# Second pass of the input projection: ScalarE copies the products out of PSUM, an accumulating DMA adds the first slab's sums

## The chip, the cores and the metric

The kernel runs on one core of a Trainium2 chip. The metric is the device time of one execution in microseconds. Before the change it was 2701.43 us, the median of 3 runs (2699.49 to 2702.08). The profile is of one more execution, which took 2703.73 us; the span that it shows, from the first to the last instruction, is 2701.6 us. What lies around the span is thus 2.1 us.

Five engines with their own instruction queues take part. Each works through its queue in order, so an instruction that waits holds up everything behind it on that engine. PE is the matrix engine (TensorE), PEld its weight loads, DVE is VectorE, ACT is ScalarE, POOL is GpSimd and SP is SyncE, which here only issues DMAs. Matrix products land in PSUM, eight banks of 128 x 512 floats; everything else lives in SBUF or in DRAM.

## The reference

Two layers of a transformer trunk over 512 latent tokens and 256 context tokens, width 2048, in float32. Each layer normalises and modulates the tokens, projects them with one wide matrix, runs four groups of four attention heads (differential A, windowed B, neighbourhood C, QK-normed D), gates the results, and projects back:

```
n  = rms_norm(h, pre_norm_g[l]) * (1.0 + scale[:, None]) + shift[:, None]
p  = jnp.split(n @ w_in[l], split_points, axis=-1)
pc = jnp.split(nc @ w_in[l], split_points, axis=-1)
oa, oa_c = diff_attention(...); ob, ob_c = window_attention(...)
on, on_c = neighborhood_attention(...); od, od_c = qknorm_attention(...)
y = (jnp.concatenate([oa, ob, on, od], axis=-1) * jax.nn.silu(p[12])) @ w_out[l]
h = h + gate[:, None] * rms_norm(y, post_norm_g[l])
```

`n @ w_in` has an inner length of 2048 and 7168 columns. The kernel handles the columns as 56 blocks of 128: the queries, keys, values and gates of the heads.

## The kernel before, in words

**Two passes.** Of the inner length of 2048, the first half (the first slab, 8 tiles of 128) is multiplied in a first pass for all 56 blocks, two blocks at a time with seven products in place of eight. Its sums go to a DRAM tensor `part[l, b]`, 128 rows x 2 x 384 floats per block: 256 latent and 128 context tokens in each of the two halves. In the second pass (`block_slots`) the second slab is multiplied, block by block, and the first slab's sums are added; the finished block goes at once to what uses it. While the second pass goes on, the attention of heads whose blocks are complete is worked in between (`head_steps`), and so is the modulation of the next layer (`mod_steps`: VectorE's lines 441 and 443, with the tile `mraw` loaded by SP). The two second passes lie at about 508 to 1165 us (layer 0) and 1912 to 2497 us (layer 1).

**Precision.** Each float32 operand is split into a high and a low part: ScalarE copies the high part (line 292), VectorE subtracts it (line 293), and `mm3` multiplies three times (lines 301 to 303). Weights (`wr` split to `wh`, `wl`) are split up to two tiles ahead; the transposed attention weights go the same way (`PTh`, `PTl`).

**A block of the second pass** is 8 slots. In each slot three matmuls add one of 8 tiles to the block's sums for the 512 latent tokens, in PSUM bank 0 or 1 by turns (`self.lb`). The products for the 256 context tokens (`ctx_steps`, bank 2) are run four tiles at a time, in the slots that follow; in layer 1 only keys and values have them. When the last tile is in, VectorE adds the tile `c`, which already holds the sums of the first pass, and leaves the total in `c` (line 819 for the latent part, line 841 for the context part). The tile `c` was loaded from `part` by SP one block ahead (`hold`, line 796).

**What reads `c`.** `done(c, ctx)` is called right behind the addition. It depends on the block: rotary embedding on VectorE (lines 868, 862, 865) for the latent queries and keys of A and B; a permuted copy on ScalarE (line 965) for C; a square and a scaled copy on ScalarE (lines 921, 922) for D; a tanh on ScalarE (line 1017) for gates, of latent and context tokens; splits on ScalarE (lines 278, 282, 292, 295) for the context parts of queries and keys; transposes on PE, three slots later (line 1001), for values.

**What sets the order.** `drive` calls one slot after another and, behind each, the attention and modulation steps that are due; `later(n, fn)` calls a function n slots later. The instructions so written are then put in each engine's queue by a scheduler when the kernel is built, which moves those that it holds for ready ahead of others. What is quoted as order below is each engine's finished queue.

**POOL** has little to do: it adds the neighbourhood bias tables (line 1265, three additions for each C head, after SP has loaded them as `x<-in_rpb`) and a few tiles between the layers. No DMA is issued from it.

Of the kernel before, what the change touches and what calls it, by code (L numbers as in the profile page):

```python
# [10 lines left out]
F32 = mybir.dt.float32  # L11
F32R = mybir.dt.float32r
I32 = mybir.dt.int32
AF = mybir.ActivationFunctionType
ALU = mybir.AluOpType
# [3 lines left out]
P = 128  # L19
# [7 lines left out]
DEPTH = 2  # L27
# [15 lines left out]
HT = 384  # L43
# [12 lines left out]
def lat_of(x):  # L56
    return x[:, :, 0:2 * P]


def ctx_of(x):  # L60
    return x[:, :, 2 * P:HT]
# [16 lines left out]
def fit(ap, like):  # L78

    return ap.rearrange("p (h t) -> p h t", h=like.shape[1]) if len(like.shape) == 3 else ap  # L80


class Kernel:
# [704 lines left out]

        return [lambda m=m, half=half: slot(m, half) for m in order for half in range(2)]

    def hold(self):

        if self.to_hold:
            l, b, w = self.to_hold.pop(0)
            c = self.cp.tile([P, 2, HT], F32, tag="c", bufs=4, name="c")[:, :, 0:w]
            self.nc.sync.dma_start(c, self.part[l, b, :, :, 0:w])
            self.held.append(c)

    def block_slots(self, l, n, what, b):

        with_ctx = l < DEPTH - 1 or what in "kv"
        done = self.take[n, what]
        r = {}

        def slot(c, j):
            if c == 0 and j == 0:
                self.lb ^= 1
                r["c"] = self.held.pop(0)
                self.hold()
            if j == 0:  # L810
                self.cur = self.weight()
            hi, lo = self.cur
            k = 4 * c + j
            js = slice(j * P, (j + 1) * P)
            (th, tl), _ = self.plain(k)
            self.mm3(self.bank(self.lb), hi[:, js], lo[:, js], th, tl, k == 0, k == 7)
            if k == 7:
                lat = lat_of(r["c"])
                self.nc.vector.tensor_add(lat, fit(self.bank(self.lb), lat), lat)  # L819
                done(r["c"], False)  # L820
            if j == 0:
                self.ctx_steps()
            if j == 3:
                self.pend = (hi, lo, c, r["c"], done) if with_ctx else None

        return [lambda c=c, j=j: slot(c, j) for c in range(2) for j in range(4)]

    def ctx_steps(self):

        if self.pend is None:  # L830
            return
        hi, lo, c, tile_c, done = self.pend
        out = self.bank(2, CTX)
        for j in range(4):
            k = 4 * c + j
            js = slice(j * P, (j + 1) * P)
            _, (th, tl) = self.plain(k)
            self.mm3(out, hi[:, js], lo[:, js], th, tl, k == 0, k == 7)
        if c == 1:
            ctx = ctx_of(tile_c)  # L840
            self.nc.vector.tensor_add(ctx, fit(out, ctx), ctx)
            done(tile_c, True)

    def x3(self):
        return self.ap.tile([P, SEQ], F32, tag="x3", bufs=3, name="x3")
# [436 lines left out]
    def layer(self, l):  # L1282

        tc, nc, a = self.tc, self.nc, self.a
        pairs = [(n, i) for n, u in enumerate(self.units) for i in range(len(u[3]))]
        self.tbanks, self.tb = [5, 6], 0
        f = self.first
        before = {1: f[1] + f[2], 6: self.rest + f[6] + f[5], 5: f[7], 7: f[3], 3: f[4]}
        again = self.second(self.ns2)
        slots = []  # L1290
        for p in pairs:
            hooks = (before, {}) if p == pairs[0] else ({}, again) if p == pairs[-1] else None
            slots.append(self.pair_slots(l, *p, START if p == pairs[0] else ORDER, hooks))
        self.drive(slots[0])
        if l == 0:
            self.heads_setup()
        anchors = [i.ins for i in self.anchors]

        def behind(fn):
            with tc.issue_after(anchors[0]), tc.issue_after(anchors[1]):  # L1300
                fn()

        self.drive([x for s in slots[1:-1] for x in s], [lambda fn=fn: behind(fn) for fn in self.late])
        self.drive(slots[-1])
        self.flush()
        self.stage.close()

        self.att = ExitStack()
        self.ap = self.att.enter_context(tc.tile_pool(name=f"att{l}", bufs=1, reuse_waits="tile"))
        self.mp, self.raws, self.og_open = Lent(self), 3, False  # L1310
        self.load_cst("rope_sub")
        self.take, sts = {}, {}
        for n in range(len(self.units)):
            self.unit_blocks(l, n, sts)
        self.held, self.lb, self.pend = [], 0, None
        self.to_hold = []
        for n, i in pairs:
            blocks = self.units[n][3][i]
            wide = l < DEPTH - 1 or blocks[0][0] == "k"
            self.to_hold += [(l, b, HT if wide else 2 * P) for _, b in blocks]  # L1320
        self.hold()
        mods = self.mod_steps([(l, 2, c, (0, 1) if l < DEPTH - 1 else (0,)) for c in range(4)])
        steps, left, last = [], 0, 0
        for n, (kind, h, gh, prs) in enumerate(self.units):
            if h == 0 and kind == "D":
                self.later(7, lambda: self.load_cst("rope_head"))
            if h == 0 and kind == "B":
                self.bm = self.ap.tile([P, 256], F32, tag="qd", bufs=2, name="bmask")
                nc.sync.dma_start(self.bm, a["bmask"])
            if h == 0 and kind == "C":  # L1330
                self.later(7, lambda: self.na_bias(l, 0))

            goal = left - last * (0 if n == len(self.units) - 1 else 0.25 if len(prs) > 1 else 0.6)
            now, done = [], 0
            while steps and done < goal:
                now.append(steps.pop(0))
                done += now[-1][0]
            left -= done
            nm = 0 if n < 6 else len(mods) * len(prs) // sum(len(u[3]) for u in self.units[n:])
            ms, mods = mods[:nm], mods[nm:]  # L1340
            self.drive([x for p in prs for w, b in p for x in self.block_slots(l, n, w, b)], now, ms)
            new = [x if isinstance(x, tuple) else (1, x) for x in self.head_steps(l, kind, h, gh, sts[n])]
            last = sum(w for w, _ in new)
            if n == 0:
                new.insert(0, (0.4 * last, lambda: None))
            left += sum(w for w, _ in new)
            steps += new
        self.ctx_steps()
        self.pend = None
        self.flush()  # L1350
        self.raws, self.og_open = RAWS, True
        self.tbanks, self.tb = [5], 0
        self.backlog = [fn for _, fn in steps]
# [259 lines left out]
```

## Time and profile before

| | |
|---|---|
| median of 3 runs | 2701.43 us (2699.49 to 2702.08) |
| profiled execution, its span | 2703.73 us, 2701.6 us |
| PE busy | 2591.7 us, 96% |
| DVE busy | 2187.2 us, 81% |
| ACT busy | 1285.7 us, 48% |
| POOL busy | 43.6 us, 2% |
| DMA issued by SP, moved | 408.45 MB |

The page's shares are averages over the whole span; what the second pass does is read from windows. A matmul's time overlaps the next one's, so PE can read as busy while it is not at its peak. A row "X <- Y: a, b, c" of the view of waits says that X sat idle a us in total, b times, c us at most, until Y ended.

### The profile page before, as it was taken

How to read it: one execution, taken by the hardware profiler on the slowest of the kernel's cores; microseconds unless marked ns; L12 is line 12 of the kernel's file. 1: busy time of each engine (PE TensorE's matmuls, PEld its weight loads, DVE VectorE, ACT ScalarE, POOL GpSimd, SP SyncE). 2: the span in 40 equal slices, each digit the busy share in tenths (PEclk: the TensorE clock that was granted, in tenths of full speed). 3: DMA queues.
4: the chain of work that ended last, by engine and by line, in shares of the span. 5: the costliest groups of instructions: out<-in, count | busy, mean ns of one | idle time of the engine just before them, and what ended most of it. 6: DMA issues, size and time to landing. Idle time of an engine off the chain costs nothing.

```text
span 2701.6 us, 41385 instructions
## 1 busy us (share of the span) xinstructions
PE 2591.7 (96%) x14392; PEld 2231.2 (83%) x14392; DVE 2187.2 (81%) x4480; ACT 1285.7 (48%) x2532; POOL 43.6 (2%) x42
## 2 busy tenths in 40 slices
PE   7899999999999999999999689999999999999997
PEld 1799999987888888887777479999878887888885
DVE  4899998789899888767889989887798988876524
ACT  3534343445556455546533464444455554544422
POOL 0000000000000000000010000000000000000001
PEclk9899999999999999999999789999999999999998
DMA  9455554422223334427886535444422334444632
GB/s 318 138 197 194 196 196 149 151 73 78 85 96 116 119 126 142 140 89 232 293 269 218 201 123 170 148 146 137 152 87 86 112 121 136 146 154 129 223 103 98
DMA packets 230497, 411.09 MB, mean 152 GB/s; under 512 B 25568, under 2 KB 59664, under 8 KB 229776
## 3 DMA queue, kind: packets, MB, share of 16 engines
q1 hardware_dynamic: 230288, 408.45, 46.3%
q8 instruction: 113, 1.85, 0.3%
q14 instruction: 96, 0.79, 0.1%
HBM read 348.17 MB, written 60.19 MB: 151 GB/s over the span
## 4 chain that ended last, share of the span: by engine, by line
PE 76%; DVE 11%; DMA 7%; ACT 3%; issue 2%; SPq 0%; POOL 0%; DVEq 0%; ACTq 0%; POOLq 0%
PE ps L301 23%; PE ps L302 23%; PE ps L303 22%; DMA mraw<-in_w_mod 3%; PE ps L1132 3%; DVE macc L443 2%; DVE wl L293 1%; PE ps L650 1%; PE ps L1034 1%; DMA mr<-in_w_mod 1%; DVE rt L862 1%; DVE h L1442 1%; PE ps L1035 1%; DMA wr<-in_w_out 1%; DMA wr<-ogd 1%
## 5 line engine op out<-in xcount | busy, mean ns | idle before, releaser
L301 PE MATMUL ps<-arena,wh 128*128 128x384 f32 (+2 forms) x3104 | 1050.6, 339 | 16.6 <-ACT arena L292 7.4
L302 PE MATMUL ps<-arena,wh 128*128 128x384 f32 (+2 forms) x3104 | 1038.8, 335 | 0.0
L303 PE MATMUL ps<-arena,wl 128*128 128x384 f32 (+2 forms) x3104 | 1037.7, 335 | 0.0
L292 ACT ACTIVATE wh<-wr 128x512 fp32r<-128x512 f32 x696 | 437.8, 630 | 710.1 <-PE ps L302 371.3
L301 PEld LDWEIGHTS ps<-arena,wh 128*128 128x128 f32 x3104 | 586.9, 189 | 47.5 <-ACT arena L292 8.6
L293 DVE TENSOR_TENSOR wl<-wr,wh 128x512 fp32r<-128x512 f32 x696 | 477.4, 688 | 176.3 <-ACT wh L292 163.7
L303 PEld LDWEIGHTS ps<-arena,wl 128*128 128x128 f32 x3104 | 587.0, 189 | 33.0
L302 PEld LDWEIGHTS ps<-arena,wh 128*128 128x128 f32 x3104 | 587.8, 189 | 27.4 <-DVE arena L293 1.1
L443 DVE SCALAR_TENSOR_TENSOR macc<-mraw,sc,macc 128x512 f32<-128x512 f32 x540 | 391.2, 750 | 38.3 <-DMA mraw<-in_w_mod 37.6
L302 PE MATMUL ps<-wl,arena 128*128 128x512 f32 x640 | 255.6, 399 | 9.2 <-DVE wl L293 9.1
L303 PE MATMUL ps<-wh,arena 128*128 128x512 f32 x640 | 253.0, 395 | 0.0
L301 PE MATMUL ps<-wh,arena 128*128 128x512 f32 x640 | 248.2, 397 | 0.0
L292 ACT ACTIVATE PTh<-ps 128x512 fp32r<-128x512 f32 (+2 forms) x224 | 114.2, 519 | 123.0 <-PE ps L1132 117.6
L293 DVE TENSOR_TENSOR PTl<-ps,PTh 128x512 fp32r<-128x512 f32 (+2 forms) x224 | 130.7, 591 | 34.1 <-ACT PTh L292 32.6
L302 PEld LDWEIGHTS ps<-wl,arena 128*128 128x128 f32 x640 | 120.4, 188 | 45.4 <-DVE wl L293 18.3
L303 PEld LDWEIGHTS ps<-wh,arena 128*128 128x128 f32 x640 | 120.4, 188 | 28.0
L301 PEld LDWEIGHTS ps<-wh,arena 128*128 128x128 f32 x640 | 120.2, 188 | 28.0 <-DVE c L819 0.2
L292 ACT ACTIVATE wh<-s 128x512 fp32r<-128x512 f32 x112 | 70.8, 633 | 135.2 <-PE ps L302 96.9
L1132 PE MATMUL ps<-ident,P 128*128 128x128 f32 x672 | 112.6, 274 | 2.0 <-DVE P L1069 0.7
L784 DVE TENSOR_TENSOR c<-ps,s 128x384 f32<-128x384 f32 (+1 forms) x168 | 86.5, 515 | 33.2 <-PE ps L303 24.6
L1132 PEld LDWEIGHTS ps<-ident,P 128*128 128x128 f32 x672 | 83.9, 140 | 32.3 <-ACT P L1111 5.3
L1111 ACT ACTIVATE P<-P,small 128x768 f32<-128x768 f32 (+2 forms) x96 | 79.4, 827 | 44.9 <-DVE small L1110 44.6
(262 smaller groups left out, 3196.7 us busy)
## 6 DMA issues: line engine op xcount, KB each, us to landing
wr<-in_w_in SPq DMA_DIRECT2D x448, 256.0 KB, 3.2
mraw<-in_w_mod SPq DMA_DIRECT2D x320, 256.0 KB, 3.0
wr<-in_w_out SPq DMA_DIRECT2D x192, 256.0 KB, 3.5
part<-c SPq DMA_DIRECT2D x80, 384.0 KB, 2.6
c<-part SPq DMA_DIRECT2D x80, 384.0 KB, 3.1
mr<-in_w_mod SPq DMA_DIRECT2D x32, 512.0 KB, 5.3
part<-c SPq DMA_DIRECT2D x32, 256.0 KB, 3.0
c<-part SPq DMA_DIRECT2D x32, 256.0 KB, 3.1
```

Of the source, the lines that this page charges most:

```text
L292: nc.scalar.activation(hi, src, AF.Copy)
L293: nc.vector.tensor_sub(lo, src, hi.bitcast(F32))
L301: mm(out, lh, rh, start=start, stop=False, skip_group_check=parts)
L302: mm(out, lh, rl, start=False, stop=False, skip_group_check=parts)
L303: return mm(out, ll, rh, start=False, stop=stop, skip_group_check=parts)
L443: nc.vector.scalar_tensor_tensor(acc, raw, col, acc, op0=ALU.mult, op1=ALU.add)
L650: nc.tensor.matmul(self.ps[0:2, 2 * c4 + 1 - kind, :], self.sc[:, k, :], raw, start=k == 0, stop=k == KT - 1)
L784: self.anchors[0] = V.tensor_add(c, ps, c if m in (7, 4) else r["s"])
L862: nc.vector.tensor_mul(fit(t2[o:o + hw], x), x[i:i + hw], fit(sin[i:i + hw], x))
L1034: self.nc.tensor.matmul(out, q["hd"[sub]][:, qs], kt[:, ks], start=True, stop=False)
L1111: nc.scalar.activation(Pt, Pt, AF.Copy, scale=sm)
L1132: nc.tensor.transpose(T[:, i * P:(i + 1) * P], st["P", t][:, c:c + P], self.ident)
```

## The change

In the second pass ScalarE copies the products out of PSUM into a fresh tile `c` (an activation with the function Copy) where VectorE added. Then POOL issues a DMA that adds the first slab's sums from `part` in DRAM onto `c` in SBUF (`accum_op=ALU.add`). There are 112 such copies and DMAs for latent and 80 for context tokens. `done`, with all that reads the total, is called four slots later than the copy. The early load of `c` by SP, and with it `hold` and its list, goes away.

```diff
-    def hold(self):
-        if self.to_hold:
-            l, b, w = self.to_hold.pop(0)
-            c = self.cp.tile([P, 2, HT], F32, tag="c", bufs=4, name="c")[:, :, 0:w]
-            self.nc.sync.dma_start(c, self.part[l, b, :, :, 0:w])
-            self.held.append(c)
+    def add_part(self, l, b, c, view, done, ctx):
+        self.nc.gpsimd.dma_start(view(c), view(self.part[l, b]), accum_op=ALU.add)
+        self.later(4, lambda: done(c, ctx))
...
             if c == 0 and j == 0:
                 self.lb ^= 1
-                r["c"] = self.held.pop(0)
-                self.hold()
...
             if k == 7:
+                r["c"] = self.cp.tile([P, 2, HT], F32, tag="c", bufs=4, name="c")
                 lat = lat_of(r["c"])
-                self.nc.vector.tensor_add(lat, fit(self.bank(self.lb), lat), lat)
-                done(r["c"], False)
+                self.nc.scalar.activation(lat, fit(self.bank(self.lb), lat), AF.Copy)
+                self.add_part(l, b, r["c"], lat_of, done, False)
...
-                self.pend = (hi, lo, c, r["c"], done) if with_ctx else None
+                self.pend = (hi, lo, c, r.get("c"), lambda t: self.add_part(l, b, t, ctx_of, done, True)) if with_ctx else None
...
         if c == 1:
             ctx = ctx_of(tile_c)
-            self.nc.vector.tensor_add(ctx, fit(out, ctx), ctx)
-            done(tile_c, True)
+            self.nc.scalar.activation(ctx, fit(out, ctx), AF.Copy)
+            done(tile_c)
```

**The order, place by place.** The names are those of tiles, with the numbers of this build; line numbers after the change are 4 lower from here on (line 1013 is what line 1017 was), and lines 815 and 837 are the new copies. First ACT at a gate block of a C head in layer 0. Before:

```order
L292 ACTIVATE PTh_11131<-ps_72 128x384
L292 ACTIVATE PTh_11143<-ps_72 128x256
L1017 ACTIVATE g_11154<-c_10867 128x512
L292 ACTIVATE wh_11219<-wr_11027 128x512
L1017 ACTIVATE g_11154<-c_10867 128x256
L292 ACTIVATE PTh_11196<-ps_72 128x256
L292 ACTIVATE PTh_11205<-ps_72 128x256
```

The same place of the change:

```order
L292 ACTIVATE PTh_11170<-ps_72 128x384
L292 ACTIVATE PTh_11182<-ps_72 128x256
L815 ACTIVATE c_11192<-ps_72 128x2x256
L292 ACTIVATE wh_11257<-wr_11056 128x512
L837 ACTIVATE c_11192<-ps_72 128x2x128
L1013 ACTIVATE g_11250<-c_11192 128x512
L292 ACTIVATE PTh_11231<-ps_72 128x256
L292 ACTIVATE PTh_11240<-ps_72 128x256
L1013 ACTIVATE g_11250<-c_11192 128x256
```

The copy of the latent products stands where the tanh of the gate stood, and the tanh has moved two instructions, a weight split and the copy of the context products, further back; the tanh of the context part stands two instructions behind that. Both tanhs read what the DMA has added to.

Second, ACT at the first key block of layer 0 (an A head). Before:

```order
L292 ACTIVATE wh_4950<-wr_4798 128x512
L292 ACTIVATE wh_4987<-wr_4817 128x512
L278 ACTIVATE kh_4943<-c_4894 64x256
L278 ACTIVATE kl_4944<-c_4894 64x256
L278 ACTIVATE kh_4943<-rt_4945 64x512
```

The same place of the change:

```order
L815 ACTIVATE c_4938<-ps_72 128x2x256
L292 ACTIVATE wh_4975<-wr_4817 128x512
L837 ACTIVATE c_4938<-ps_72 128x2x128
L278 ACTIVATE kh_4971<-c_4938 64x256
L278 ACTIVATE kl_4972<-c_4938 64x256
L292 ACTIVATE wh_5017<-wr_4836 128x512
```

The split of the key's context part stands right behind the copy (`L837`), with nothing between the two on this engine.

Third, POOL where the first neighbourhood table of layer 0 is added, in the change:

```order
L793 DMA c_10425<-part_96 128x2x256
L793 DMA c_10425<-part_96 128x2x128
L1261 ISA
L1261 TENSOR_TENSOR cst_10736<-cst_10736,x3_10735 128x384
L793 DMA c_10586<-part_96 128x2x256
L1261 TENSOR_TENSOR cst_10736<-cst_10736,x3_10735 128x256 x2
L793 DMA c_10586<-part_96 128x2x128
L793 DMA c_10732<-part_96 128x2x256
```

Before, the table additions were alone in this queue; now the adding DMAs stand before, between and behind them.

More of the change, by code (lines that the diff above doesn't have):

```diff
@@ L1314, in layer @@
             self.unit_blocks(l, n, sts)
[L1315 to L1321, printed above, removed]
+        self.lb, self.pend = 0, None
         mods = self.mod_steps([(l, 2, c, (0, 1) if l < DEPTH - 1 else (0,)) for c in range(4)])
```

## The prediction

> **What bounds the kernel now.** I read the page first, then the second pass by windows, since only that stage changes. The two windows are layers 0 and 1; the columns are their length and each engine's busy time.
>
> ```profile
> core 0: us, PE busy (x) PEld busy (x) DVE busy (x) ACT busy (x) POOL busy (x), PEclk, DMA share, GB/s
> 508.00:1165.00 657.00, 647.92 (x3858) 553.03 (x3857) 563.50 (x1367) 346.24 (x735) 9.20 (x9) 1.00 0.35 112
> 1912.00:2497.00 585.00, 575.12 (x3146) 475.85 (x3146) 479.72 (x1024) 302.06 (x589) 10.98 (x12) 1.00 0.39 124
> ```
>
> PE bounds the second pass: it is idle for 657 - 647.9 = 9.1 us and 585 - 575.1 = 9.9 us, 19 us together. DVE is busy 1043 of 1242 us (84%), ACT 648 us (52%). So the whole gain open to a lighter DVE is what PE loses by waiting, not DVE's own time. Who ended PE's idle time, by the view of waits (layer 0, then layer 1):
>
> ```profile
> PE ps L984 <- DVE x L976: 1.5, 2, 0.8
> PE ps L302 <- DVE PTl L293: 1.2, 2, 0.7
> PE ps L301 <- DVE g L1166: 0.3, 1, 0.3
> ...
> PE ps L302 <- DVE PTl L293: 1.2, 2, 0.9
> PE ps L301 <- DVE c L841: 0.7, 1, 0.7
> PE ps L1132 <- DVE P L1069: 0.7, 1, 0.7
> ```
>
> These come to 5.6 us; the larger rows beside them end with ACT, which the change loads more.
>
> **What is removed.** The additions, as groups of the view by lines:
>
> ```profile
> L819 DVE TENSOR_TENSOR c<-ps,c 128x512 f32<-128x512 f32 x112 | 76.8, 685 | 19.2 <-PE ps L303 18.4 <-DMA wr<-in_w_in 0.2
> L841 DVE TENSOR_TENSOR c<-ps,c 128x256 f32<-128x256 f32 x80 | 33.4, 418 | 6.5 <-PE ps L303 5.6
> ```
>
> That is 110 us off DVE, which leaves it 933 of 1242 us (75%). On the path of PE I take 6 us of gain, the sum of the waits that DVE ended. Bounds: nothing, or all 19 us of idle, and as much again that the busy figure can hide (a matmul of 0.39 us follows its forerunner after 0.23 us, in the timeline below, so a gap of up to 0.16 us doesn't show): 0 to -38 us.
>
> SP issues 112 loads fewer. SP is not waited for by anything long, and each load was a block ahead; I take nothing. If some of the other loads gain from the freed queue, it is inside the bound above.
>
> **What is added on ACT.** The copies have the shape of copies out of PSUM that ACT makes already:
>
> ```profile
> L292 ACT ACTIVATE PTh<-ps 128x512 fp32r<-128x512 f32 x60 | 34.9, 594 | 27.2 <-PE ps L1132 27.0
> L292 ACT ACTIVATE PTh<-ps 128x256 fp32r<-128x256 f32 x38 | 14.5, 382 | 23.8 <-PE ps L1132 20.3 <-PE ps L303 2.5 <-DVE small L514 0.9
> ```
>
> 112 x 0.594 + 80 x 0.382 = 97 us: ACT goes to 745 of 1242 us, 60%. What hides it is ACT's own idle time, nearly half of the pass; without that cover it would cost its 97 us. I take nothing, since ACT's copy takes the place of DVE's addition in the same chain and is 0.04 to 0.09 us shorter.
>
> **The new wait.** Before, the tile was loaded a block ahead, and the total was there when the addition ended. Now three things stand between the last product and the reader: the copy, POOL's issue, and a DMA that reads DRAM and the tile and writes the tile. The trace of before has no DMA from POOL and none that adds. The nearest rows are SP's (size, and median us from issue to landing):
>
> ```profile
> c<-part SPq DMA_DIRECT2D x32, 256.0 KB, 3.1
> h<-h SPq DMA_DIRECT2D x16, 256.0 KB, 6.8
> cst<-in_rope_sub SPq DMA_DIRECT2D x2, 512.0 KB, 4.2
> cst<-in_rope_head SPq DMA_DIRECT2D x2, 512.0 KB, 3.5
> n<-cnd SPq DMA_DIRECT2D x16, 64.0 KB, 1.8
> n<-cnd SPq DMA_DIRECT2D x8, 128.0 KB, 2.9
> ```
>
> The same 256 KB from the same tensor took 3.1 us as a plain load. The adding DMA handles them twice, which makes the 512 KB rows the nearest: 3.5 and 4.2 us. I take 4.2, POOL's issue included; the bounds are the shortest and the longest landing here, 1.8 and 6.8 us. The Trainium skill, "DMA: Bandwidth & Descriptors", section "Anatomy of one DMA — SWDGE (gpsimd) path", puts a DMA issued by GpSimd at about 2.0 us plus its bytes over 436 KB per us, an estimate of 2.6 us for this one; the plain load's 3.1 us already exceeds it, and by it the sum that ends below at 2766 would come to some 2720 us.
>
> How much time the order leaves is read by laying the changed queue against the timeline of before, at the gate block of the C head that the order shows:
>
> ```profile
> 1070.46 0.39 PE L303 MATMUL ps<-arena,wl 128*128 128x512 f32 x1
> 1070.69 0.39 PE L301 MATMUL ps<-arena,wh 128*128 128x512 f32 x1
> 1071.71 0.64 ACT L1017 ACTIVATE g<-c 128x512 f32<-128x512 f32 x1 [1.67 <-DVE c L819]
> 1072.87 0.63 ACT L292 ACTIVATE wh<-wr 128x512 fp32r<-128x512 f32 x1 [0.53 <-PE ps L302]
> 1073.45 0.42 ACT L1017 ACTIVATE g<-c 128x256 f32<-128x256 f32 x1
> 1074.32 0.39 ACT L292 ACTIVATE PTh<-ps 128x256 fp32r<-128x256 f32 x1 [0.45 <-PE ps L1132]
> ```
>
> The block's last product ends at 1070.46 + 0.39 = 1070.85. The tanh now stands behind the weight split, which ends at 1073.50. The window is 2.65 us. Needed are 0.59 + 4.2 = 4.8 us, so ACT waits 2.1 us at the tanh. Behind it in ACT's queue are the two `PTh` splits, for which DVE and then PE wait, and the next weight split. With a landing of 1.8 us there would be no wait (2.4 against 2.65), with 6.8 us one of 4.7 us.
>
> The four slots of delay written in the code don't give four slots of time, since the scheduler has moved readers forward to where it held the sum for ready. Counted over both layers in the order: of 112 latent sums, 68 are first read on ACT, 60 of them with at most 8 ACT instructions between copy and reader (4 is the median), 28 on DVE (the rotary products), 16 on PE some seven slots later. Of 80 context sums, 56 are first read on ACT, 52 of them that close, and at the first key block with none between. I count one wait a block, since the first pushes the engine back by more than the second still lacks: 60 blocks, and half of the 28 that DVE reads, whose places are wider: 74 blocks x 2.1 us = 155 us of waiting.
>
> **What PE pays of it.** The trace has waits of this kind: DVE stood still for a late `mraw`. The rows of those waits, and windows of 4 us from the start of each on:
>
> ```profile
> 1127.17 0.75 DVE L443 SCALAR_TENSOR_TENSOR macc<-mraw,sc,macc 128x512 f32<-128x512 f32 x1 [3.77 <-DMA mraw<-in_w_mod]
> ...
> 1123.20:1127.20 4.00, 4.00 (x27) 3.58 (x26) 0.23 (x2) 0.63 (x1) 0.00 (x0) 1.00 0.84 254
> 1127.20:1131.20 4.00, 3.82 (x26) 3.17 (x24) 4.00 (x8) 1.02 (x3) 0.00 (x0) 1.00 0.52 190
> 1131.20:1135.20 4.00, 2.63 (x14) 2.33 (x15) 3.99 (x10) 2.67 (x6) 0.00 (x0) 1.00 0.41 133
> ...
> 2263.40:2267.40 4.00, 4.00 (x22) 3.32 (x21) 1.81 (x6) 1.48 (x4) 0.00 (x0) 1.00 0.43 140
> 2267.40:2271.40 4.00, 2.85 (x14) 2.14 (x13) 3.87 (x9) 2.31 (x5) 0.00 (x0) 1.00 0.19 63
> ```
>
> PE goes on while DVE waits (27 matmuls, fully busy), and pays 4 to 8 us later, when it comes to what DVE had not done: 0.18 + 1.37 = 1.55 us after a wait of 3.77 us, 41%. In layer 1 a shorter wait of about 2.2 us, from 2263.4 on (DVE busy 1.81 of 4 us), cost 1.15 us, 52%. ACT has more idle time in which to catch up than DVE had, so I take the lower share: 155 x 0.41 = 64 us. Bounds: 0, and 96 blocks x 4.7 x 0.52 = 235 us.
>
> **POOL's queue.** The adding DMAs stand in order among the table additions:
>
> ```profile
> 1038.97 2.33 POOL L1265 TENSOR_TENSOR cst<-cst,x 128x256 f32<-128x256 f32 x2
> ```
>
> A DMA behind two of them is 2.3 us late. Eight C heads make 8 x 2.3 x 0.41 = 8 us, if each catches a reader that is already waiting. A table addition that itself waits for its `rpb` loads holds the DMA longer; that belongs to the second rival.
>
> **The sum.** Against the profiled execution, 2703.7 us: -6 (DVE) + 64 (waits) + 8 (POOL) = 2769.7. The profiled execution stood 2.3 us over the median of the runs, which leaves 2767; I write 2766, 2.4% over the median.
>
> **Rivals.** First, *the DMA is hidden and DVE's relief shows* (faster). If the sum lands within about 2.6 us of the last product, or PE's backlog of matmuls covers the waits as it covered the first 8 us after the wait at 1123 us, only the gain is left: -6 to -38 us, 2664 to 2695, about 2685. For it speaks that PE stays fully busy through single waits; against it that such waits would now come every 11 to 12 us (1242 us over 112 blocks), so that a backlog is not rebuilt, and that even the plain load needs 3.1 us. It decides from a landing of about 2 us on downwards.
>
> Second, *POOL becomes the bound of the second pass* (much slower). All 192 DMAs and 24 table additions go through one queue in order; if a DMA holds POOL until it has landed, or is issued slowly, its own 6.8 us and the one ahead of it add up, and the wait per block is that of the upper bound: 74 x 4.7 x 0.41 = 143 us and more, 2840 to 2940. The profile has only POOL's 2% of busy time to set against it, and no row of a DMA from POOL.
>
> Third, *the two cancel*: waits of a few tenths, by a landing of 2.9 us (need 3.5, wait 0.85, 74 x 0.85 x 0.41 = 26 us), against a gain of the same size hidden in PE's busy time. That leaves 2701 us.
>
> **How the numbers follow.** The forecast, waits that PE pays in part, has 0.55, with its own range of 2715 to 2810; the first rival 0.21, the second 0.15, the third 0.09. From 2685 to 2850 the range leaves out half of the first rival and half of the second, under 2 in 10. A measurement of this kernel tells about 0.2% from no change. Faster: 0.21, the first rival; same: 0.09, the third; slower: 0.70.
>
> **What would show it.** The page should have DVE near 2077 us and ACT near 1383 us, whatever the time is. Right, if the view of waits names the DMA `c<-part` ahead of ACT's tanh, permuted copies and splits and of DVE's first rotary product, with 1 to 3 us each and some 150 us in all, if those DMAs land 3.5 to 5 us after their issue, and if PE's idle time in the second pass grows from 19 us to 60 or more, ended mostly by ACT and DVE work that came behind these waits. The first pass and the output phase should keep their lengths. Wrong, if the waits sum to under 50 us (first rival), if POOL's rows show DMAs queued behind each other (second), or if ACT's copies themselves hold PE's banks.

## The result, and the profile after

The changed kernel takes 2954.1 us (median of 4 runs, 2949.09 to 2959.57) against 2700.5 us for the kernel before in the same comparison: a ratio of 1.0941, with a 95% interval of 1.0912 to 1.097. The forecast was 2766 us with a range of 2685 to 2850. The direction was right, and the size was missed by 188 us, nearly three quarters of the 254 us that the change costs.

The page of the kernel after, its engines, POOL's adding DMAs as a group, and their landing (size, median us from issue to landing):

```profile
PE 2671.8 (91%) x14392; PEld 2282.3 (77%) x14392; DVE 2115.1 (72%) x4288; ACT 1360.7 (46%) x2724; POOL 252.7 (9%) x234
...
L793 POOL DMA_DIRECT2D c<-part x192 | 211.6, 1102 | 2348.1 <-ACT c L815 1126.2
...
c<-part POOLq DMA_DIRECT2D x112, 256.0 KB, 4.5
c<-part POOLq DMA_DIRECT2D x80, 128.0 KB, 3.5
```

DVE lost 72 us of busy time and ACT gained 75, in the direction of the change but less than the 110 and 97 us that the forecast took: it had DVE near 2077 us and ACT near 1383. The forecast added up the records' durations, and busy time counts once what two records overlap; added up, the records of DVE are 102 us less and those of ACT 94 us more. PE, with the same 14392 matmuls, is busy 80 us longer than before (2591.7). POOL is busy 9%, so its own work bounds nothing.

The second passes by windows, each from the first to the last matmul of 512 columns of the pass. (The forecast's window for layer 0 ended at 1165 us, 46 us before the pass does.) First the kernel before, layers 0 and 1 (length, then the busy time of PE, PEld, DVE, ACT and POOL, then the granted clock):

```profile
505.50:1211.44 705.94, 696.02 (x4145) 594.32 (x4144) 596.98 (x1438) 370.55 (x789) 11.62 (x12) 1.00 0.34 109
1915.13:2494.47 579.34, 569.46 (x3110) 470.92 (x3109) 475.46 (x1016) 298.51 (x580) 10.98 (x12) 1.00 0.39 123
```

The same of the kernel after:

```profile
505.72:1341.98 836.26, 738.78 (x4146) 621.38 (x4145) 558.19 (x1328) 410.77 (x899) 131.40 (x122) 0.96 0.41 92
2053.20:2733.41 680.21, 603.93 (x3109) 492.95 (x3108) 444.93 (x937) 332.25 (x659) 97.12 (x91) 0.95 0.45 105
```

The two passes are 130.3 and 100.9 us longer, 231 us in all. The two output phases behind them grew by 11 and 7 us; the rest kept its length within 4 us. The 231 us are of two kinds. PE is idle 173.8 us in place of 19.8, which is 154 us more. And it is busy 1342.7 us in place of 1265.5 for the same matmuls, which is 77 us more. The granted clock, 1.00 before, is 0.96 and 0.95 here: by the clock's record 71.7 and 64.9 us of the two passes ran at half clock, and half of that, 68 us, is work that took longer. The other 9 of the 77 us are not accounted for; the ends of matmuls are modelled in the profile.

Who waited for the DMA, by groups of one shape each in the kernel after (busy time and mean ns; idle time ahead of the group and what ended it). The first four read latent sums, the other six context sums:

```profile
L1013 ACT ACTIVATE g<-c 128x512 f32<-128x512 f32 x32 | 20.1, 629 | 73.5 <-DMA c<-part 72.5 <-DMA ogd<-g 0.9
L961 ACT ACTIVATE x<-c 128x256 f32<-128x256 f32 x48 | 17.8, 410 | 44.0 <-DMA c<-part 36.1 <-issue 7.9
L917 ACT ACTIVATE x<-c 128x512 f32<-128x512 f32 x12 | 7.5, 624 | 8.4 <-DMA c<-part 8.2
L864 DVE TENSOR_TENSOR rt<-c,cst 128x512 f32<-128x512 f32 x28 | 19.4, 692 | 50.1 <-DMA c<-part 50.0
L1013 ACT ACTIVATE g<-c 128x256 f32<-128x256 f32 x16 | 6.7, 416 | 32.2 <-DMA c<-part 32.1
L292 ACT ACTIVATE kh<-c 128x256 fp32r<-128x256 f32 x12 | 5.0, 416 | 31.0 <-DMA c<-part 31.0
L278 ACT ACTIVATE kh<-c 64x256 fp32r<-64x256 f32 x8 | 3.3, 417 | 41.5 <-DMA c<-part 41.5
L295 ACT ACTIVATE qh<-c 128x256 fp32r<-128x256 f32 x8 | 3.3, 416 | 11.3 <-DMA c<-part 11.3
L917 ACT ACTIVATE x<-c 128x256 f32<-128x256 f32 x8 | 3.3, 412 | 6.4 <-DMA c<-part 6.4
L282 ACT ACTIVATE qh<-c 64x256 fp32r<-64x256 f32 x4 | 1.7, 416 | 18.7 <-DMA c<-part 18.7
```

The latent readers waited 166.8 us, in 70 waits of 2.4 us (46 on ACT, 24 on DVE); the context readers 141.0 us, in 46 waits of 3.1 us. That is 308 us on ACT and DVE, twice what the forecast had.

One block shows how a wait reaches PE. This is the timeline of the kernel after at a gate block of layer 0 (start, duration, engine and line; in brackets the idle time ahead and what ended it):

```profile
1073.95 0.60 ACT L815 ACTIVATE c<-ps 128x512 f32<-128x512 f32 x1 [0.84 <-PE ps L303]
...
1074.96 1.10 POOL L793 DMA_DIRECT2D c<-part  x1 [11.14 <-ACT c L815]
...
1076.47 0.36 ACT L837 ACTIVATE c<-ps 128x256 f32<-128x256 f32 x1
...
1079.14 0.63 ACT L1013 ACTIVATE g<-c 128x512 f32<-128x512 f32 x1 [2.30 <-DMA c<-part]
1079.43 1.11 POOL L793 DMA_DIRECT2D c<-part  x1 [3.37 <-issue]
1079.67 0.64 ACT L292 ACTIVATE PTh<-ps 128x256 fp32r<-128x256 f32 x2
...
1080.09 0.39 PE L301 MATMUL ps<-PTh,vh 128*128 128x256 f32 x1 [1.89 <-ACT PTh L292]
```

The copy ends at 1074.55 and POOL starts the DMA 0.41 us later. It lands at 1079.14, where ACT's tanh has stood for 2.30 us. The split `PTh` is queued behind the tanh, and PE stands 1.89 us for the split. A second thing is to be seen: the context copy ends at 1076.83, but POOL starts the context DMA only at 1079.43, just behind the landing of the latent one.

What follows in PE is read from four windows of 3.41 us around that place (the clock is the third number from the right):

```profile
1074.59:1078.01 3.42, 3.42 (x26) 3.02 (x24) 1.29 (x2) 0.90 (x2) 1.10 (x1) 1.00 0.62 133
1078.01:1081.42 3.41, 1.52 (x10) 1.15 (x9) 1.36 (x3) 1.17 (x3) 1.11 (x1) 1.00 0.42 108
1081.42:1084.83 3.41, 3.41 (x15) 3.13 (x15) 0.71 (x2) 0.42 (x1) 0.00 (x0) 0.50 0.30 36
1084.83:1088.25 3.42, 3.42 (x21) 3.02 (x21) 1.85 (x5) 0.85 (x2) 0.00 (x0) 1.00 0.40 144
```

In the period of the stall PE is busy 1.52 of 3.41 us. The next period runs at half clock and makes 15 matmuls, where the one before the stall made 26. So a stall of 1.89 us is followed by a period that loses up to 1.7 us more, half of its length.

### The profile page after: what moved, and what is told of

It reads as the page before. It is cut to its first block, busy times and chain, and to the rows that moved or that the text cites. A ratio compares the mean times of both kernels' runs of the same rounds, so it can differ in the third digit from the quotient of the medians.

```text
span 2947.4 us, 41572 instructions
## 1 busy us (share of the span) xinstructions
PE 2671.8 (91%) x14392; PEld 2282.3 (77%) x14392; DVE 2115.1 (72%) x4288; ACT 1360.7 (46%) x2724; POOL 252.7 (9%) x234
## 3 DMA queue, kind: packets, MB, share of 16 engines
q0 software_dynamic: 52224, 39.86, 10.0%
## 4 chain that ended last, share of the span: by engine, by line
PE 36%; DMA 14%; issue 13%; DVE 9%; ACT 5%; POOL 2%; SPq 0%; DVEq 0%; POOLq 0%; ACTq 0%
PE ps L302 11%; PE ps L301 11%; PE ps L303 11%; DMA c<-part 9%; DMA mraw<-in_w_mod 4%; DVE macc L443 2%; POOL c L793 2%; DVE wl L293 1%; PE ps L1128 1%; ACT c L815 1%; DVE h L1432 1%; ACT P L1094 1%; DVE rt L858 1%; DVE small L1084 1%; ACT wh L292 0%
## 5 line engine op out<-in xcount | busy, mean ns | idle before, releaser
L301 PE MATMUL ps<-arena,wh 128*128 128x384 f32 (+2 forms) x3104 | 1064.1, 343 | 22.2 <-ACT arena L292 7.4
L302 PE MATMUL ps<-arena,wh 128*128 128x384 f32 (+2 forms) x3104 | 1052.2, 339 | 0.0
L303 PE MATMUL ps<-arena,wl 128*128 128x384 f32 (+2 forms) x3104 | 1051.3, 339 | 0.0
L301 PEld LDWEIGHTS ps<-arena,wh 128*128 128x128 f32 x3104 | 599.2, 193 | 58.0 <-ACT arena L292 8.6
L303 PEld LDWEIGHTS ps<-arena,wl 128*128 128x128 f32 x3104 | 598.7, 193 | 35.1 <-DVE wl L293 0.2
L302 PEld LDWEIGHTS ps<-arena,wh 128*128 128x128 f32 x3104 | 598.9, 193 | 30.9 <-DVE arena L293 1.1
L793 POOL DMA_DIRECT2D c<-part x192 | 211.6, 1102 | 2348.1 <-ACT c L815 1126.2
L302 PEld LDWEIGHTS ps<-wl,arena 128*128 128x128 f32 x640 | 121.5, 190 | 47.0 <-DVE wl L293 19.8
L301 PE MATMUL ps<-kh,qh 128*128 128x256 f32 (+2 forms) x216 | 76.4, 354 | 65.6 <-ACT P L1094 61.9
```

The source lines that it names most:

```text
L301: mm(out, lh, rh, start=start, stop=False, skip_group_check=parts)
L302: mm(out, lh, rl, start=False, stop=False, skip_group_check=parts)
L303: return mm(out, ll, rh, start=False, stop=stop, skip_group_check=parts)
L793: self.nc.gpsimd.dma_start(view(c), view(self.part[l, b]), accum_op=ALU.add)
```

## The experiments

My theory at the outset: the loss is the adding DMA's time to its landing, which shows at readers that stand too early in the in-order queues; PE pays a part at once, and the clock adds to it. Three rivals: the DMA's traffic or its issue on POOL (A), ScalarE's copies (B), the delay of four slots and the order that comes of it (C).

| run | time, us | against before (95%) |
|---|---|---|
| after | 2954.1 | 1.0941 (1.0912 to 1.097) |
| x1 copies, no DMA, no delay | 2712.1 | 1.0028 (1.0015 to 1.0041) |
| x2 no DMA | 2705.2 | 1.0006 (0.9996 to 1.0017) |
| x3 DMA to an unread tile | 2705.1 | 1.0004 (0.9994 to 1.0015) |
| x4 before, with the delay | 2701.8 | 0.9994 (0.9983 to 1.0005) |
| x5 eight slots in the code | 2948.3 | 1.0908 (1.0889 to 1.0927) |
| x6 two slots in the code | 2967.2 | 1.0981 (1.0941 to 1.1022) |
| x7 plain loads from POOL | 2772.4 | 1.0257 (1.0242 to 1.0273) |
| x8 adding DMAs of 16 KB | 2793.4 | 1.0336 (1.0319 to 1.0352) |
| x9 readers held, six slots | 2808.5 | 1.0385 (1.0368 to 1.0403) |
| x10 readers held, eight slots | 2793.1 | 1.0334 (1.0312 to 1.0357) |
| x11 readers held, ten slots | 2805.0 | 1.0372 (1.0354 to 1.0389) |
| x12 all readers held, eight slots | 2751.0 | 1.0164 (1.0138 to 1.0189) |
| x13 the same, no DMA | 2715.4 | 1.0041 (1.0029 to 1.0053) |
| x14 only latent DMAs add | 2867.8 | 1.0613 (1.0586 to 1.064) |
| x15 only context DMAs add | 2816.6 | 1.0415 (1.0396 to 1.0433) |

### The parts of the change, one without the other

The copies alone, with the readers at once:

```diff
-        self.nc.gpsimd.dma_start(view(c), view(self.part[l, b]), accum_op=ALU.add)
-        self.later(4, lambda: done(c, ctx))
+        done(c, ctx)
```

> The kernel after, without the accumulating DMA and without the delay of four slots: ScalarE copies the products out and their readers follow at once. It leaves out the first slab's sums. Theory (readers wait for the adding DMA's landing, and TensorE waits behind them): nothing is left to wait for, so 2680 to 2715 us, against 2954 with the DMA, TensorE idle in the second passes 15 to 35 us, and no 128x512 product at less than the full clock there. Rival A (the DMA's traffic or its issue on GpSimd is what costs): the same 2680 to 2715. Rival B (ScalarE's 192 copies fill its queue and hold PSUM banks): 2800 to 2950, for the copies are all still there. Rival C (the four slots of delay turn the order round): 2680 to 2715.

The copies and the delay, without the DMA (only the line of the DMA goes):

> The kernel after without the accumulating DMA, but with the copies on ScalarE and the delay of four slots. It leaves out the first slab's sums. Theory: 2685 to 2720 us, within 15 us of the copies alone. Rival A: the same. Rival B: 2800 to 2950. Rival C (delay): 2800 to 2950, where the copies alone without the delay come to about 2700.

The DMAs are there, but nobody reads what they write (the edit also makes the spare tile `scr`):

```diff
-        self.nc.gpsimd.dma_start(view(c), view(self.part[l, b]), accum_op=ALU.add)
+        self.nc.gpsimd.dma_start(view(self.scr), view(self.part[l, b]), accum_op=ALU.add)
```

> The kernel after, with every accumulating DMA, of the same size and at the same place on GpSimd, but into a spare tile that nobody reads (to make room, the tiles of products rotate over three buffers and not four). The first slab's sums are left out of what follows. Theory: within 20 us of the kernel without the DMA, 2690 to 2735 us, because nothing waits for the landing; the landing itself still takes 3.5 to 4.7 us. Rival A (traffic, GpSimd, the addition in the DMA engines): nearly all of the 253 us stays, 2880 to 2960.

The kernel before, with the delay of four slots:

```diff
-                done(r["c"], False)
+                self.later(4, lambda: done(r["c"], False))
...
-            done(tile_c, True)
+            self.later(4, lambda: done(tile_c, True))
```

> The kernel before, with VectorE's additions where they were, but with the readers of the sums four slots later, as in the kernel after. It computes all. Theory: 2695 to 2720 us, since the delay by itself makes nobody wait. Rival C (delay and the order that comes of it): 2800 or more.

All four came out at 2702 to 2712 us. B and C fall: the copies and the delay cost nothing, or 0.28% where the readers follow at once. The third run makes all 192 adding DMAs, and they land even later than in the kernel after:

```profile
scr<-part POOLq DMA_DIRECT2D x112, 256.0 KB, 5.0
scr<-part POOLq DMA_DIRECT2D x80, 128.0 KB, 4.3
```

Its second passes are those of the kernel before, at full clock:

```profile
504.54:1214.48 709.94, 700.73 (x4145) 594.54 (x4144) 552.20 (x1328) 413.11 (x899) 54.72 (x52) 1.00 0.33 89
1918.88:2497.32 578.44, 570.81 (x3109) 471.08 (x3108) 440.51 (x937) 331.67 (x659) 33.85 (x33) 1.00 0.35 101
```

But this is no clean test of A. The spare tile is filled by no copy, so the DMAs don't wait for the copies, and the issue on POOL has moved: only 59 of the 192 start inside the two second passes (POOL has 52 and 33 instructions there, against 122 and 91 in the kernel after). The rest run in the first passes, as the pages' rows of POOL show (busy tenths in 40 slices, first the kernel after, then this one):

```profile
POOL 0000000111111111120010000000111111112001
POOL 0011212222000000000010002212210000000001
```

A is bounded by a later pair: in x12 below all but three of the 192 start inside the second passes, and it is 36 us slower than its twin x13 without the DMA, so that traffic and issue cost 36 us at most. The scheduler has also put the queues of x2 and x3 in another order than those of the kernel after, so these runs don't price the waits by themselves; x7, in the same order, and x12 do. They do show that there was nothing to gain: with VectorE relieved and no DMA at all (x2), the kernel is not faster than before.

### How late the readers are: the delay in the code, and the time to landing

The delay in the code, once doubled (with attention steps a fifth of a unit later, so that keys and queries are there when the scores need them) and once halved:

```diff
-        self.later(4, lambda: done(c, ctx))
+        self.later(8, lambda: done(c, ctx))
```

> The kernel after with eight slots between the copy and the readers in place of four; so that the keys and queries are there in time, the attention steps of each unit begin a fifth of a unit later. It computes all. Theory (price = how late the sums are for their readers): in the profile of after a block of the second pass costs 836.5 us / 64 blocks against 706 / 64 before, 2.06 us more over all 112 blocks; four slots more are about 3.2 us, which covers that: 2700 to 2745 us, waits that name the landing under 60 us in all (308 before this edit), half-clock periods in the second passes under 15 us. Rival (the landing costs wherever the readers stand, or the clock stays low for another reason): 2880 to 2960.

> The kernel after with two slots between the copy and the readers in place of four. It computes all. Theory: readers stand two slots, about 1.6 us, earlier, so 112 x 1.6 = 180 us more less what the order takes in: 3060 to 3160 us, with more half-clock periods than after has (130 us in the second passes). Rival (one wait a block of a size that the place of the readers does not set): 2940 to 2980.

The same DMA from POOL without the addition, all engines in the order of after; and the addition cut to 16 columns:

```diff
-        self.nc.gpsimd.dma_start(view(c), view(self.part[l, b]), accum_op=ALU.add)
+        self.nc.gpsimd.dma_start(view(c), view(self.part[l, b]))
```

> The kernel after with the same DMA from GpSimd at the same place, but without the addition: it loads the first slab's sums over the copied products, so the second slab's products are left out. All engines' instructions stand in the order of after. Theory: only the time from issue to landing counts; with L us in place of the 4.5 us for 256 KB the time is 2954 - 112 x (4.5 - L), give or take 30 us: 2925 to 2960 if the addition costs nothing in the DMA, 2840 if a plain load lands in 3.5 us. Rival (the addition itself, reading and writing the tile, is what disturbs the other engines): under 2800 with L still over 4.

```diff
-        self.nc.gpsimd.dma_start(view(c), view(self.part[l, b]), accum_op=ALU.add)
+        self.nc.gpsimd.dma_start(view(c)[..., 0:16], view(self.part[l, b])[..., 0:16], accum_op=ALU.add)
```

> The kernel after with each accumulating DMA cut to the first 16 columns of each half (16 KB in place of 256 or 128 KB). It leaves out the rest of the first slab's sums. Theory: the landing falls to some 2 to 3 us, of which 1.1 us is the issue on GpSimd; readers four slots behind the copy are then 0 to 0.5 us late: 2700 to 2770 us. Rival (a fixed cost of each DMA from GpSimd, or of the wait, whatever the size): 2880 to 2960.

Both expectations on the delay were missed: four slots more took off 6 us where 209 to 254 were expected (the waits stayed at 306 us, where under 60 were expected), two slots fewer added 13 where 106 to 206 were. The finished queues say why. In ScalarE's queue the first reader of a latent sum stands 4 instructions behind the copy, in the median, with two slots, with four, and with eight. The scheduler puts a reader where it holds the sum for ready, whatever slot the code calls it in.

The time to landing does count. The plain loads:

```profile
c<-part POOLq DMA_DIRECT2D x112, 256.0 KB, 3.3
c<-part POOLq DMA_DIRECT2D x80, 128.0 KB, 2.8
```

With the same order on every engine, plain loads, which land 1.2 us (latent) and 0.7 us (context) sooner, take off 182 us. That was more than the 1.2 x 112 = 134 us of my expectation (its 2820 us against 2772). And the small adding DMAs, which land sooner still, came out 23 us above their expected range and are slower than the plain loads by 21 us, which the landing alone can't give. (The scheduler ordered this kernel a little differently from the kernel after, so part of the 21 us may be the order.)

```profile
c<-part POOLq DMA_DIRECT2D x192, 16.0 KB, 2.8
```

### Readers moved back in the queues

Since the delay in the code didn't move the readers, the next kernels tell the scheduler to put them behind the last projection matmul of a later slot. It is an ordering when the queues are made, with no wait on the chip:

```diff
+    def behind(self, done, c, ctx):
+        traced = self.nc.cur_bb.bb.instructions
+        n = len(traced)
+        done(c, ctx)
+        how = mybir.DependencyInfo(mybir.DependencyClass.NoSync, mybir.DependencyReason.DATA)
+        for i in traced[n:]:
+            self.tc.add_manual_dep(i, self.last_mm.name, how, reason="behind")
...
-        self.later(4, lambda: done(c, ctx))
+        self.later(6, lambda: self.behind(done, c, ctx))
```

> The kernel after, computing all, with the readers held back in the finished queues: a reader of the sums is placed no earlier than the last projection matmul of the sixth slot behind the copy (an ordering for the scheduler only, without a wait on the chip), and attention steps begin a tenth of a unit later. In ScalarE's queue the first reader of a latent sum then stands 8 instructions behind the copy in the median, against 4 in after and also 4 with two or eight slots of delay written in the code. Theory (price = landing less the time the finished queues leave; the earlier miss with eight slots came of the scheduler, which put the readers back): most waits go, 2740 to 2830 us, half-clock time in the second passes under 50 us. Rival (whoever uses the sums comes late all the same, so the wait moves from the reader to the heads behind it): 2900 to 2970.

> The same with eight slots, and attention steps a fifth of a unit later: first reader 11 instructions behind the copy in the median. Theory: 2705 to 2760 us, waits that name the landing under 60 us in all. Rival: 2900 to 2970.

> The same with ten slots, and attention steps six tenths of a unit later: first reader 17 instructions behind the copy in the median. Theory: nearly no waits for the landing (under 20 us), and a time set by the copies and the order alone, 2700 to 2760 us, where the upper end is what the later attention steps leave over for the output phase. Not below 2690 in any case, since the kernel without the DMA took 2705. Rival: 2900 to 2970.

Holding the readers back takes off 146 to 161 us, so their place in the queue is what makes the landing dear. Six slots came out in the expected range, but the two longer holds stopped 33 and 45 us above theirs, with waits of 67 and 59 us where under 60 and under 20 were expected, and ten slots were no better than eight. In the kernel with eight slots the view of who waited for the DMA has one large row left (us, times), and with ten slots the same line has 48 us:

```profile
  DVE rt L866: 52.1, 25
```

Line 866 is the rotary product against the sine, which `rope` calls through `later`, so that the edit had not held it. The scheduler had put it ahead of the product against the cosine, which was held. The next kernel holds these calls back too, and its twin leaves out the DMA in nearly the same order:

```diff
     def later(self, n, fn):
+        if self.mm_held is not None:
+            fn = lambda f=fn, mm=self.mm_held: self.behind(f, mm)
         self.delayed.append([n, fn])
```

> The kernel after, computing all, with every reader of the sums held back by eight slots, also the rotary products against the sine, which the kernel held before had left where the scheduler put them (they waited 52 us for the landing in 25 waits there). Theory: with these waits gone the exponentials that came late behind VectorE are in time, and 2715 to 2760 us are left, against 2793. Rival (what is left is the price of the held order and of the later attention steps, not of waits): 2780 to 2800.

> The same kernel with the accumulating DMA taken out, in nearly the same order on every engine. It leaves out the first slab's sums. Theory: within 25 us of the kernel with the DMA, 2700 to 2735 us, as the landing is then no longer waited for in either. Rival (order): 2770 to 2800, as with the DMA. A gap of over 40 us between the two would say that the landing still costs although its readers stand later.

2751 us, inside the theory's range. Who waited for the DMA in this kernel:

```profile
  ACT g L1025: 16.0, 7
  DVE rt L876: 3.6, 1
  ACT kh L280: 2.7, 3
  ACT qh L284: 0.8, 1
```

23 us of waiting are left of 308, with a landing that has not changed (4.4 us), and the second passes are nearly what they were, with the clock at 1.00 and 0.99:

```profile
508.74:1224.73 715.99, 701.43 (x4145) 595.60 (x4144) 551.92 (x1326) 409.58 (x897) 131.84 (x122) 1.00 0.47 108
1942.82:2538.46 595.64, 575.11 (x3109) 472.91 (x3108) 438.73 (x936) 331.42 (x658) 97.39 (x91) 0.99 0.50 120
```

Four fifths of the loss, 203 of 254 us, are gone by the readers' place. Of the 48 us that remain over the kernel before, 12 are the order and the later attention steps (the twin, 2715 us). 36 us come with the DMA, more than the 25 that I expected as the most. By the two profiles 23 us lie in the second passes and 16 in the output phases (the profiled executions are 41 us apart). That the output phases lengthen was seen in every kernel that waits for the landing, but the first of them is also 6 us longer in x4, which has no adding DMA; the cause stays open. None of the kernels beats the one before, and the two in these orders without the DMA, x2 and x13, are not faster than it either.

### Do adding DMAs wait for one another?

That 16 KB which land in 2.8 us cost more than 256 KB which land in 3.3 us suggests something else. POOL's timeline has it. In the kernel after, the second DMA of a block:

```profile
518.00 1.12 POOL L793 DMA_DIRECT2D c<-part  x1 [3.50 <-issue]
...
553.61 1.11 POOL L793 DMA_DIRECT2D c<-part  x1 [3.76 <-issue]
```

With plain loads, same order:

```profile
523.39 0.73 POOL L793 DMA_DIRECT2D c<-part  x1 [0.33 <-issue]
...
549.56 0.72 POOL L793 DMA_DIRECT2D c<-part  x1 [1.56 <-ACT c L837]
```

"Issue" is time in which POOL waits for nothing that the profile shows. Over the whole kernel after, no two of the 192 adding DMAs start less than 3.65 us apart; the closest plain loads start 0.93 us apart; adding DMAs of 16 KB 2.79 us, about their landing. None of the 192 starts before the one ahead of it has landed, the closest 0.26 us after; of the plain loads, 43 do. To price it, all four combinations in one order:

```diff
-        self.nc.gpsimd.dma_start(view(c), view(self.part[l, b]), accum_op=ALU.add)
+        self.nc.gpsimd.dma_start(view(c), view(self.part[l, b]), **({} if ctx else dict(accum_op=ALU.add)))
```

> The kernel after, in the same order on all engines, where only the 112 DMAs of latent products add and the 80 of context products are plain loads from GpSimd (these leave out the second slab's products of the context tokens). In the profile of after, no two adding DMAs start within 3.6 us of each other, although the context copy is done 2 us after the latent one; with plain loads the closest two start 0.9 us apart. Theory of the queue (an adding DMA is not started before the one ahead of it has landed, so the context part comes 2.5 us late): with only one kind that adds, nothing stands behind anything, 2790 to 2860 us. Theory without the queue (each adding DMA costs by its own longer landing, 4.5 against 3.3 and 3.5 against 2.8 us): 2870 to 2910 us here.

> The reverse: the context DMAs add, the latent ones are plain loads (these leave out the second slab's products of the latent tokens), same order on all engines. Plain loads for both took 2772 us, adding for both 2954 us, 182 us apart. Theory of the queue: 2780 to 2820 us, and the excesses of this and its sister over 2772 sum to under 110 us. Theory without the queue: 2815 to 2860 us, and the two excesses sum to 160 to 200 us.

Where only one kind adds, DMAs again start within 1 us of one another at the closest: the gap is there only where an adding DMA follows an adding DMA. The excesses over the plain loads are 95 us (latent) and 44 us (context), 139 us in sum, against 182 us where both add. The runs don't decide between the two expectations: x14 lies between the two ranges, x15 where they overlap, and the sum between under 110 and 160 to 200. So 139 us of the 182 come with one kind or the other, and some 42 us only where both add. The split is rough, since the context DMAs land in 3.0 us in x14 and in 4.2 us in x15, not in 2.8 and 3.5. The queueing of adding DMAs behind one another is the difference that the traces show there; since a wait costs nothing up to a point and more than its length where the clock falls, some of the 42 us may be that the two costs don't simply add.

The context waits tell how much the queueing matters there. Where both add they are 46 waits of 141 us; in x15, where context DMAs add but no adding one stands ahead, 47 waits of 107 us; in x14, with plain context loads, 29 waits of 46 us. So the queueing gives some 34 of the 141 us, and the larger part comes without it. The rows of x15 for the context splits of A's keys and queries, whose latent sums DVE reads (us, times; in the kernel after 41.5 and 18.7 us):

```profile
  ACT kh L278: 30.3, 8
...
  ACT qh L282: 11.5, 4
```

## Why the prediction was right or wrong

**Direction and mechanism: right.** The DMA is waited for by ACT's tanh, permuted copies and splits and by DVE's first rotary product, in the rows named, and PE pays behind them. Copies at no cost on ACT were right (x2). The first pass kept its length; the output phases did not.

**DVE's relief, -6 us: nothing.** Without the DMA the time is that of before (x2). DVE was busy 84% of the second pass and still kept PE waiting for under 6 us, by the rows that the prediction shows.

**Landing, 4.2 us with POOL's issue: 0.7 us short.** Measured are 4.5 us, and 0.41 us from the copy's end to POOL's start in the block shown. By the step's own window that makes a wait of 0.59 + 4.9 - 2.65 = 2.8 us, where 2.1 was taken. The Trainium skill, "DMA: Bandwidth & Descriptors", section "Anatomy of one DMA — SWDGE (gpsimd) path", gives, as an estimate from its figures, 2.6 us for 256 KB. The runs have 3.3 us for a plain load from POOL and 4.5 us for one that adds, so it was right to let the rows decide, and even they were too low.

**"One wait a block": the step that failed first.** For the latent sums the total held: 74 waits of 2.1 us were predicted, 155 us, and 70 of 2.4 us came, 167 us. The number of waits is luck in its parts, since 60 were expected on ACT and 14 on DVE, and 46 and 24 came. What failed is the reason given for leaving out the context sums, that "the first pushes the engine back by more than the second still lacks". In 20 of the 56 blocks whose context sum ACT reads first, the queries and keys of A and B, the latent sum is read by DVE, so that no first wait pushes ACT back: 19 of these readers waited, 81 us together. In the other 36 blocks both readers are on ACT, and there 27 more waits came, 60 us. With plain context loads (x14) these shrink to 9 us, near what the step had assumed; with adding ones they don't, and where both add, the second DMA isn't started before the first has landed. The forecast had that idea in its second rival, a DMA that "holds POOL until it has landed", and the sign that it named, DMAs queued behind each other in POOL's rows, was seen. But the rival tied it to POOL being the bound, and POOL is at 9%.

**PE's share, 0.41: the step that failed second.** The second passes grew by 231 us for 308 us of waiting, 0.75. As idle time it is 154 of 308, 0.50, near the 52% of the second place that the step had read and not taken. The other 77 us are longer matmul time, 68 of them at half clock by the clock's record, a term that the sum didn't have. It couldn't be read from the second passes before, where the clock never fell and PE's longest wait was 1.6 us. Nor is the share one number: with plain loads (x7), 145 us of waiting, close to the 155 of the forecast, make the second passes 66 us longer, 0.45. So the forecast's share nearly fits waits of its own sum, and was far too low where they doubled.

**Output phases, put at no change: 18 us.** The sum thus had 64 us for the waits where 231 were measured, and nothing for the output phases where 18 were; why these lengthened stays open.

**The signs.** The landing of 3.5 to 5 us came as named. The single waits, named at 1 to 3 us, were 1.6 to 3.2 us in the mean of each group but for 5.2 and 4.7 us at the context parts of A's keys and queries. The waits were to sum to some 150 us and came to 308, and PE's idle time was to grow to 60 us or more and came to 174.

**The range** ended at 2850. The upper bound of 235 us for the waits would just have held the second passes' growth, but by luck: it was made of 96 waits of 4.7 us at a share of 0.52, and 116 waits of 2.7 us at 0.75 came. The range was cut back to half of the second rival, and the result lies outside that rival's 2840 to 2940 too.

**POOL's table additions, +8 us,** were not measured apart.

## What to carry to other kernels

When a sum that an engine finished in place is handed to a DMA, count every reader of every part, and look at where the finished queues put the reader, not at the delay in the code: here two, four and eight slots in the code gave the same place and 2967, 2954 and 2948 us. Look also at which engine reads each part: a wait on one engine doesn't hold back a reader on another. PE's idle time alone can understate what stalls cost (here 154 us idle, 231 us in all); read the granted clock beside it. And before moving work off an engine, see who waits for it: DVE at 84% had nothing to give back.

## What the runs showed of the hardware

**The clock went with PE's busy share, period by period.** I counted the second passes and the first pass of layer 1 of eleven profiles (before, after, x2, x3, x5 to x11) in periods of 3.41 us, the grid on which the clock's record changes. After a period in which PE was busy less than 45%, the next was at half clock in 142 of 144 cases; from 45 to 55%, in 18 of 74; above that, in 27 of 5295. The Trainium skill, "TensorE: Matmul & The Clock Gate", section "HAM oscillation — how this bites in real kernels", gives the rule of no PE-idle gaps over about 3.4 us. By that rule the stall of 1.89 us shown above would have cost its own length and no more. The traces differ: with idle time of somewhat over half a period, the next was nearly always at half clock. The counts are of what happened beside each other; no run set the busy share by itself.

**Adding DMAs from POOL go one at a time.** Starts at least 3.65 us apart (128 and 256 KB) and 2.79 us (16 KB), none before the one ahead has landed, where plain loads from the same queue start as little as 0.93 us apart. Behind a plain load an adding DMA doesn't wait, nor the reverse: in x15 43 and in x14 68 of the 192 DMAs start before the one ahead has landed. The adding ones also hold POOL for 1.10 us each against 0.73, need 1.2 us more to land 256 KB, and come in 52224 packets where the plain ones of the same bytes come in 12800. Where the wait for one another sits, in POOL's program or in the DMA engines, the traces don't show.
